# Writing the end of an output projection bank by bank, moving a table load, and adding squares before their row sums

## The chip, the cores and the metric

The kernel runs on 1 core of one Trainium2 chip. The metric is the device time of one execution in microseconds (us). A core has engines that run their own queues in order and wait for each other through semaphores: PE (matrix products, with PEld its weight loads), DVE (VectorE), ACT (ScalarE), POOL (GpSimd) and SP, which here only starts transfers.

## The reference, cut to what matters

Two model blocks follow each other over 256 tokens of width 1024. The first (attention, mLSTM, mixture of experts) is not touched by the change. The second has two layers; layer 0 is a gated linear attention ("gla"), layer 1 a state space layer ("s5"). Three places of it matter:

```
# layer 0: each of the 4 heads has 512 output columns; they are normed per token and head
o = gla_chunked(q, k, v, g)                       # (B, L, 4, 512)
o = o * rsqrt(mean(o * o, over 512) + EPS) * out_norm_w

# layer 1, after the state space scan (y is 256 x 2048)
y = gelu(y)
y = y * sigmoid(y @ w_glu + b_glu)                # w_glu 2048 x 2048
seq_out = y
...
y = concatenate([seq_out, xa]) * silu(z)          # 256 x 3072
x = x + y @ w_out                                 # w_out 3072 x 1024
return x * rsqrt(mean(x * x) + EPS) * final_norm_w
```

## The kernel before, in words

Everything is held transposed: features on the 128 partitions, the 256 tokens (T) along the free axis. A weight matrix comes in tiles of 1 MB (`load`, L262, issued by SP), and each half of a tile is split into a rounded part and a rest (`split`, L267 on ACT writes `whi`, L268 on DVE or POOL writes `wlo`); a product is then three passes through PE (`mm3`), left and right rounded part and both cross terms. Such products stand at L280, since `mm` records every one of them. The split halves rotate through four buffers (`ws`), the raw tiles through five. Sums pile up in PSUM, in eight banks that are handed out anew from stage to stage (`psum_banks`); the first product into a bank handed out anew waits until whoever read it last is done.

**The heads of layer 0** (L1518 to L1532). For each head `f` and each of its four blocks `e` of 128 columns, PE forms the block `po` in a bank (two products, `ps<-gatt,gv`), ACT squares it (`sq`, L1524) and DVE copies it out (L1525, into `gqk`, `gz` or `gG` by head). A product of the constant matrix `mean` with each square (`ps<-sq,c_ident`) adds the four up over the partitions in a bank `pm`. ACT takes the root (`gro`, L1528), DVE its reciprocal (L1529) and multiplies the four blocks by it (L1531). Behind the last head the banks are handed out anew and the projection `gx` starts (`ps<-hh,whi`).

**The output stage of layer 1** (from L1740). For each of eight groups PE applies the output table (`st<-Xs,tab`), DVE adds (L1747), ACT applies gelu (L1748), and the result goes out to DRAM and back in another order (`yd`, `yy`), is split again, and waits as an operand of `w_glu`. Between these PE already multiplies the tiles f = 16 to 23 of the output projection (`wout`, `acc<-gyh,whi` and the like: 24 products a tile, into four banks `acc`). Then for f = 0 to 15: 48 products of `w_glu` into a bank `ps`, ACT the sigmoid (L1781), DVE a product with the gate (L1782), the split into `gyh` and `gyl` (two buffers each), and one tile of the output projection, one f behind (`last`). Each tile goes through all four banks.

**The end.** When `acc` is complete, DVE adds each of the eight column blocks to the residual (L1792), ACT squares it (`yy`, L324), PE sums the squares (`st<-c_ident,yy`), POOL scales the block by the norm's weight (L1794); ACT takes the root (`rfc`, L333), DVE the reciprocal, PE spreads it over the partitions (`ps<-c_ident,rfc`), DVE multiplies (L1799) and four transfers take the result out.

`root_table` is a one-element root on ACT, whose only use is that ACT loads the table for roots at that place. A scheduler, not the order of the text alone, decides where each instruction stands in its engine's queue: what depends on nothing may stand far ahead. `tc.issue_after` holds the instructions in it behind a given one.

## Time and profile before

| what | value |
|---|---|
| time, median of 3 runs | 1500.61 us (1500.07 to 1500.84) |
| the profiled execution | 1499.36 us |
| its span, first to last instruction | 1497.3 us |
| PE busy | 1337.9 us (89%) |
| DVE busy | 761.6 us (51%) |
| ACT busy | 549.8 us (37%) |
| POOL busy | 323.3 us (22%) |
| mean granted clock of PE | 0.93 |

The span is read in stretches: the heads of layer 0 run from about 863 to 889 us, the output stage of layer 1 from about 1290 us, its loop over f from about 1345 us, and the end from about 1477 us. Busy shares over the whole span mix stages with different limits. Between the span and the time of the execution lie 2.1 us; the profiled execution lies 1.25 us below the median.

### The profile page before, as it was taken

The numbers are of one execution on the slowest core, as the hardware profiler recorded it, in microseconds if no ns is written. First come the engines' busy times: TensorE is split into PE (matmuls) and PEld (weight loads), VectorE is DVE, ScalarE is ACT, GpSimd is POOL, SyncE is SP. The second block draws the span as 40 slices with busy tenths as digits, with TensorE's granted clock in tenths as the row PEclk, the third lists the DMA queues.
The fourth block names the chain that finished last, engine by engine and source line by source line (L and its number), as shares of the span: only waits on it lengthen the run. The fifth ranks groups of instructions, "written<-read, shape, count | busy, mean of one in ns | idle before, by whom it ended". The sixth has DMA issues, their size and how long they took to land. (4 is left out here: it accounts for less than half of the span.)

```text
span 1497.3 us, 25797 instructions
## 1 busy us (share of the span) xinstructions
PE 1337.9 (89%) x10632; PEld 1065.1 (71%) x10632; DVE 761.6 (51%) x1498; ACT 549.8 (37%) x859; POOL 323.3 (22%) x450
## 2 busy tenths in 40 slices
PE   5999998987887888686679999999999999999997
PEld 2777796553454555341159989999888988999997
DVE  2766454812233321010047686588846899665553
ACT  3754553321211122110034435644522355444443
POOL 0031121412223231200008887111400000030001
PEclk8899999998988999896689999999999999999998
DMA  9776764999999999999994525889766534675540
GB/s 364 277 268 250 268 246 174 379 400 420 420 408 415 420 408 420 420 421 374 421 370 156 204 92 178 259 251 320 265 203 204 170 138 147 213 205 189 178 141 29
DMA packets 87626, 414.86 MB, mean 277 GB/s; under 512 B 26432, under 2 KB 28016, under 8 KB 43472
## 3 DMA queue, kind: packets, MB, share of 16 engines
q1 hardware_dynamic: 66768, 381.85, 66.9%
q0 software_dynamic: 8016, 22.13, 4.7%
q10 hardware_dynamic: 12720, 9.18, 1.9%
q8 instruction: 86, 1.41, 0.4%
q14 instruction: 36, 0.29, 0.1%
HBM read 392.90 MB, written 20.22 MB: 276 GB/s over the span
## 5 line engine op out<-in xcount | busy, mean ns | idle before, releaser
L267 ACT ACTIVATE whi<-w 128x1024 fp32r<-128x1024 f32 x252 | 263.7, 1056 | 329.8 <-PE ps L280 249.9
L268 DVE TENSOR_TENSOR wlo<-w,whi 128x1024 fp32r<-128x1024 f32 x222 | 273.4, 1240 | 145.2 <-ACT whi L267 144.6
L280 PE MATMUL ps<-hh,whi 128*128 128x256 f32 x928 | 272.8, 294 | 11.2 <-DVE zt L1614 5.0
L280 PE MATMUL ps<-hh,wlo 128*128 128x256 f32 x928 | 266.9, 288 | 2.0 <-DVE wlo L268 1.8
L280 PE MATMUL ps<-hl,whi 128*128 128x256 f32 x928 | 267.8, 289 | 0.9 <-DVE hl L1579 0.7
L280 PEld LDWEIGHTS ps<-hh,whi 128*128 128x128 f32 x928 | 179.0, 193 | 19.5 <-issue 9.1
L280 PEld LDWEIGHTS ps<-hh,wlo 128*128 128x128 f32 x928 | 178.8, 193 | 4.5 <-DVE wlo L268 2.6
L280 PEld LDWEIGHTS ps<-hl,whi 128*128 128x128 f32 x928 | 179.0, 193 | 2.0 <-DVE hl L1579 0.7
L280 PE MATMUL A<-w,xg 128*32 128x512 f32 x984 | 139.6, 667 | 33.8 <-DMA w<-in_w 32.9
L280 PE MATMUL acc<-gyl,whi 128*128 128x256 f32 x384 | 109.1, 284 | 0.6 <-DVE gyl L268 0.6
L280 PE MATMUL acc<-gyh,wlo 128*128 128x256 f32 x384 | 109.1, 284 | 0.0
L280 PE MATMUL acc<-gyh,whi 128*128 128x256 f32 x384 | 108.2, 282 | 0.0
L268 POOL TENSOR_TENSOR wlo<-w,whi 128x1024 fp32r<-128x1024 f32 x30 | 70.6, 2368 | 167.1 <-ACT whi L267 166.9
L934 DVE SCALAR_TENSOR_TENSOR xT<-m,mod,xT 128x256 f32<-128x256 f32 x64 | 27.8, 480 | 142.7 <-PE m L280 142.7
L280 PEld LDWEIGHTS A<-w,xg 128*32 128x32 f32 x984 | 23.8, 114 | 102.3 <-DMA w<-in_w 73.2
L280 PE MATMUL A<-w,gT 128*32 128x512 f32 x512 | 75.0, 687 | 24.1 <-DMA w<-in_w 16.5
L960 DVE TENSOR_TENSOR g<-g,A 128x512 f32<-128x512 f32 x8 | 5.5, 687 | 134.3 <-PE A L280 134.3
L280 PEld LDWEIGHTS acc<-gyl,whi 128*128 128x128 f32 x384 | 72.7, 189 | 1.5 <-DVE gyl L268 0.8
L280 PEld LDWEIGHTS acc<-gyh,whi 128*128 128x128 f32 x384 | 73.2, 191 | 0.2 <-issue 0.2
L280 PEld LDWEIGHTS acc<-gyh,wlo 128*128 128x128 f32 x384 | 72.9, 190 | 0.2 <-issue 0.2
L1759 POOL TENSOR_TENSOR zs<-zs,yy 128x256 f32<-128x256 f32 x16 | 14.7, 935 | 236.9 <-DMA yy<-yd 236.1
L280 PE MATMUL ps<-wlo,hh 128*128 128x256 f32 x192 | 56.1, 292 | 3.4 <-DVE wlo L268 3.4
(585 smaller groups left out, 2766.8 us busy)
## 6 DMA issues: line engine op xcount, KB each, us to landing
w<-in_w SPq DMA_DIRECT2D x187, 1024.0 KB, 11.5
w<-in_wada SPq DMA_DIRECT2D x24, 1024.0 KB, 7.3
w<-in_wo SPq DMA_DIRECT2D x24, 1024.0 KB, 5.3
w<-in_sglu SPq DMA_DIRECT2D x16, 1024.0 KB, 4.9
w<-in_gz SPq DMA_DIRECT2D x12, 1024.0 KB, 6.9
w<-in_sz SPq DMA_DIRECT2D x12, 1024.0 KB, 4.8
w<-in_win SPq DMA_DIRECT2D x10, 1024.0 KB, 7.1
w<-in_xk SPq DMA_DIRECT2D x8, 1024.0 KB, 9.7
```

Of the source, the lines that this page charges most:

```text
L267: self.nc.scalar.activation(hi, src, AF.Copy)
L268: (eng or self.nc.vector).tensor_sub(lo, src, hi.bitcast(F32))
L280: self.nc.tensor.matmul(ps, l, r, start=start, stop=stop, **kw)
L934: self.nc.vector.scalar_tensor_tensor(self.xT[:, f], pc[:, T * c:T * c + T], self.m(5)[:, f:f + 1], self.xT[:, f], op0=OP.mult, op1=OP.add)
L960: nc.vector.tensor_mul(g1, g1, p3)
L1759: nc.gpsimd.tensor_mul(zs[:, f], zs[:, f], u)
```

## The change

In the heads, the squares of one head are added up on DVE (three additions for four squares), and one product with `mean` per head takes the place of four. In the loop over f, the tiles f = 13, 14 and 15 of the output projection are held back until the last `w_glu` product and then written bank by bank, tile 15 one bank behind the others; their weights stay split (one half of them in the buffer `xa`), and `gyh` and `gyl` get a third buffer. `root_table` is held behind the last sigmoid.

```diff
--- before.py
+++ after.py
@@ -268,12 +268,15 @@
         (eng or self.nc.vector).tensor_sub(lo, src, hi.bitcast(F32))
         return hi, lo
 
-    def halves(self, src):
+    def halves(self, src, room=None):
 
         raw = self.load(src.rearrange("p a b c -> p (a b c)") if len(src.shape) == 4 else src.rearrange("p a b -> p (a b)"))
         for i in range(2):
-            hi = self.ws.tile([128, 1024], F32R, tag="whi", name="whi")
-            lo = self.ws.tile([128, 1024], F32R, tag="wlo", name="wlo")
+            if i and room is not None:
+                hi, lo = room[:, 0], room[:, 1]
+            else:
+                hi = self.ws.tile([128, 1024], F32R, tag="whi", name="whi")
+                lo = self.ws.tile([128, 1024], F32R, tag="wlo", name="wlo")
             yield self.split(raw[:, 1024 * i:1024 * i + 1024], hi, lo, self.nc.gpsimd if i < self.spread else None)
 
     def mm(self, ps, l, r, start, stop, **kw):
@@ -1383,6 +1386,12 @@
             cs = slice(128 * c, 128 * c + 128)
             self.mm3(o, [x[:, cs] for x in w], y, first and c % 2 == 0, last and c % 2 == 1, skip_group_check=True)
 
+    def wout_bank(self, acc, g, w, y, last):
+
+        for c in range(2):
+            cs = slice(256 * g + 128 * c, 256 * g + 128 * c + 128)
+            self.mm3(acc[g][:, T * c:T * c + T], [x[:, cs] for x in w], y, False, last and c == 1, skip_group_check=True)
+
     def gated(self, W, s, z):
 
         nc = self.nc
@@ -1520,10 +1529,14 @@
                     po = self.psum()[:, :T]
                     self.mm(po, v[:, 0, es], att[:, f, 0:256], True, False, skip_group_check=True)
                     self.mm(po[:, 128:], v[:, 1, es], att[:, f, 256:384], False, True, skip_group_check=True)
-                    sq = self.t(W, [128, T], "sq")
+                    sq = self.t(W, [128, T], "sq" if e else "gro")
                     nc.scalar.activation(sq, po, AF.Square)
                     nc.vector.tensor_copy(o[:, e], po)
-                    self.mm(pm, self.cp["mean"], sq, e == 0, e == 3)
+                    if e:
+                        nc.vector.tensor_add(sums, sums, sq)
+                    else:
+                        sums = sq
+                self.mm(pm, self.cp["mean"], sums, True, True)
                 ro = self.t(W, [128, T], "gro")
                 nc.scalar.activation(ro, pm, AF.Sqrt, bias=self.eps, scale=2.0)
                 nc.vector.reciprocal(ro, ro)
@@ -1761,13 +1774,18 @@
 
             def last(f, g, wo=[None]):
                 if f % 2 == 0:
-                    wo[0] = self.halves(io["wo1"][f // 2])
+                    wo[0] = self.halves(io["wo1"][f // 2], self.t(P, [128, 2, 1024], "xa", F32R) if f == 12 else None)
+                if f == 12:
+                    self.wout(acc, next(wo[0]), g, False, False)
+                    kept.append(next(wo[0]))
+                    return
                 self.wout(acc, next(wo[0]), g, f == 16, f == 15)
 
-            prev = None
+
+            prev, kept, lasty = None, [], []
             for f in (16, 17, 18, 19, 20, 21, 22, 23, 0, 1, 2, 3, 4, 5, 6, 7, 8, 9, 10, 11, 12, 13, 14, 15):
-                gh = self.t(W, [128, T], "gyh", F32R)
-                gl = self.t(W, [128, T], "gyl", F32R)
+                gh = self.t(W, [128, T], "gyh", F32R, bufs=3)
+                gl = self.t(W, [128, T], "gyl", F32R, bufs=3)
                 if f >= 16:
                     self.split(xa[:, f - 16], gh, gl)
                     last(f, (gh, gl))
@@ -1778,15 +1796,23 @@
                         self.mm3(ps, [x[:, 128 * k:128 * k + 128] for x in wg], [x[8 * (k % 2) + 4 * j + k // 2] for x in ys],
                                  j + k == 0, j + k == 8)
                 sg = self.t(W, [128, T], "sg")
-                nc.scalar.activation(sg, ps, AF.Sigmoid, bias=self.v("s5_b_glu_2", f))
+                gate = nc.scalar.activation(sg, ps, AF.Sigmoid, bias=self.v("s5_b_glu_2", f))
                 nc.vector.tensor_mul(sg, sg, zs[:, f])
                 self.split(sg, gh, gl)
                 if f == 15:
-                    self.root_table(W)
-                if prev:
+                    with tc.issue_after(gate.ins):
+                        self.root_table(W)
+                if prev and f < 14:
                     last(*prev)
+                if f >= 13:
+                    lasty.append((gh, gl))
                 prev = f, (gh, gl)
-            last(*prev)
+            kept += list(self.halves(io["wo1"][7]))
+            for g in range(5):
+                for i in range(3):
+                    b = g - (i == 2)
+                    if 0 <= b < 4:
+                        self.wout_bank(acc, b, kept[i], lasty[i], i == 2)
             ps = self.psum("st")[:, :2].rearrange("p (t n) -> p t n", t=2)
             for k in range(8):
                 nc.vector.tensor_add(x3[:, k], acc[k // 2][:, T * (k % 2):T * (k % 2) + T], x3[:, k])
```

On DVE, around the second head. `gqk0` and `gqk1` hold the blocks of heads one and two, `gz` those of head three; `ps_...` are banks, `gro` is a sum of squares or a root.

Before:

```order
L1529 RECIPROCAL gro_7430<-gro_7430 128x256
L1525 COPY gqk1_7398<-ps_7445 128x256
L1531 SCALAR_TENSOR_TENSOR gqk0_7397<-gqk0_7397,vec_74,gro_7430 128x256 x4
L1525 COPY gqk1_7398<-ps_7452 128x256
L1525 COPY gqk1_7398<-ps_7459 128x256
L1529 RECIPROCAL gro_7466<-gro_7466 128x256
```

After:

```order
L1542 RECIPROCAL gro_7430<-gro_7430 128x256
L1534 COPY gqk1_7398<-ps_7438 128x256
L1544 SCALAR_TENSOR_TENSOR gqk0_7397<-gqk0_7397,vec_74,gro_7430 128x256 x4
L1534 COPY gqk1_7398<-ps_7444 128x256
L1536 TENSOR_TENSOR gro_7441<-gro_7441,sq_7447 128x256
L1534 COPY gqk1_7398<-ps_7451 128x256
L1536 TENSOR_TENSOR gro_7441<-gro_7441,sq_7454 128x256
L1534 COPY gqk1_7398<-ps_7458 128x256
L1536 TENSOR_TENSOR gro_7441<-gro_7441,sq_7461 128x256
L1542 RECIPROCAL gro_7466<-gro_7466 128x256
```

Three additions have come in, the last of them directly ahead of the reciprocal of the same head. (Before, the head's first copy stands ahead of the first row shown.)

On PE, the last head and the first product of the projection behind it. In brackets stands whom the instruction waits for (DVE_49 is DVE, Activation_49 is ACT, PE_49 is PE itself).

Before:

```order
L280 MATMUL ps_7524<-gatt_6552,gv_6828 128x256 [waits DVE_49]
L280 MATMUL ps_7524<-gatt_6552,gv_6828 128x128
L280 MATMUL ps_7509<-sq_7520,c_ident_72 128x256 [waits Activation_49]
L280 MATMUL ps_7531<-gatt_6552,gv_6828 128x256
L280 MATMUL ps_7509<-sq_7527,c_ident_72 128x256 [waits Activation_49]
L280 MATMUL ps_7531<-gatt_6552,gv_6828 128x128
L280 MATMUL ps_7509<-sq_7534,c_ident_72 128x256 [waits Activation_49]
L280 MATMUL ps_7550<-hh_6437,whi_7553 128x256 [waits DVE_49,Activation_49]
```

After:

```order
L283 MATMUL ps_7473<-gro_7477,c_ident_72 128x256 [waits DVE_49,PE_49]
L283 MATMUL ps_7510<-gatt_6552,gv_6828 128x256 [waits PE_49]
L283 MATMUL ps_7510<-gatt_6552,gv_6828 128x128
L283 MATMUL ps_7516<-gatt_6552,gv_6828 128x256 [waits PE_49]
L283 MATMUL ps_7516<-gatt_6552,gv_6828 128x128
L283 MATMUL ps_7523<-gatt_6552,gv_6828 128x256 [waits Activation_49]
L283 MATMUL ps_7523<-gatt_6552,gv_6828 128x128
L283 MATMUL ps_7530<-gatt_6552,gv_6828 128x256 [waits PE_49]
L283 MATMUL ps_7530<-gatt_6552,gv_6828 128x128
L283 MATMUL ps_7509<-gro_7513,c_ident_72 128x256 [waits DVE_49,PE_49]
L283 MATMUL ps_7550<-hh_6437,whi_7553 128x256 [waits Activation_49]
```

The products with squares now come once a head, behind all its blocks and ahead of the next head's, and wait for DVE instead of ACT.

At the end, ACT from the last sigmoid on and PE's last rows. `rfc` is the root of the final norm, `st` the bank of its sums.

Before, ACT and then PE:

```order
L1781 ACTIVATE sg<-ps,vec 128x256
L267 ACTIVATE gyh<-sg 128x256
L324 ACTIVATE yy<-xT 128x256 x8
L333 ACT_TABLE_LOAD
L333 ACTIVATE rfc<-st,c_ident 128x2
L280 MATMUL acc<-gyh,wlo 128x256
L280 MATMUL st<-c_ident,yy 128x1 x16
L280 MATMUL ps<-c_ident,rfc 128x128 x2
```

After, ACT and then PE:

```order
L1799 ACTIVATE sg<-ps,vec 128x256
L342 ACT_TABLE_LOAD
L342 ACTIVATE root<-c_ident 128x1
L267 ACTIVATE gyh<-sg 128x256
L327 ACTIVATE yy<-xT 128x256 x8
L336 ACTIVATE rfc<-st,c_ident 128x2
L283 MATMUL acc<-gyh,wlo 128x256
L283 MATMUL st<-c_ident,yy 128x1 x16
L283 MATMUL ps<-c_ident,rfc 128x128 x2
```

The table load has moved from behind the squares to between the last sigmoid and the split that follows it (before, `root_table` had stood ahead of the first gelu); on PE the sums of squares stand behind all of `acc` as before.

## Rows read from the trace of the kernel before

**Rows 1.** The page's busy times over the whole span (engine, us busy, share, instructions).

```profile
PE 1337.9 (89%) x10632; PEld 1065.1 (71%) x10632; DVE 761.6 (51%) x1498; ACT 549.8 (37%) x859; POOL 323.3 (22%) x450
```

**Rows 2.** Busy time of each engine by stretch of the heads of layer 0: stretch, its length, busy us of PE, PEld, DVE, ACT and POOL with instructions, granted clock of PE (1.00 is 2.4 GHz, 0.50 is 1.2 GHz), share of DMA, GB/s.

```profile
878.00:884.00 6.00, 6.00 (x32) 4.97 (x31) 6.00 (x12) 2.71 (x7) 5.76 (x14) 1.00 0.07 25
884.00:890.00 6.00, 2.89 (x13) 2.25 (x12) 6.00 (x11) 0.86 (x2) 3.53 (x9) 0.85 0.22 87
```

**Rows 3.** DVE's instructions in order of time in the heads: start, us (of merged ones from the first's start to the last's end), line, operation, tile, count. An idle time would stand in brackets.

```profile
871.12 1.40 DVE L1525 COPY gqk<-ps 128x256 f32<-128x256 f32 x4
872.55 1.23 DVE L268 TENSOR_TENSOR wlo<-w,whi 128x1024 fp32r<-128x1024 f32 x1
873.69 0.42 DVE L1525 COPY gqk<-ps 128x256 f32<-128x256 f32 x1
...
885.99 1.69 DVE L1531 SCALAR_TENSOR_TENSOR gz<-gz,vec,gro 128x256 f32<-128x256 f32 x4
887.60 1.07 DVE L1525 COPY gG<-ps 128x256 f32<-128x256 f32 x3
888.60 1.74 DVE L1529 RECIPROCAL gro<-gro 128x256 f32<-128x256 f32 x1
```

**Rows 4.** PE's products in order of time, in the heads and at the start of the projection behind them (in brackets the idle time before a row and what ended it).

```profile
869.77 0.59 PE L280 MATMUL ps<-sq,c_ident 128*128 128x256 f32 x2
870.20 1.04 PE L280 MATMUL ps<-gatt,gv 128*128 128x128 f32 x6
...
885.55 0.70 PE L280 MATMUL ps<-sq,c_ident 128*128 128x256 f32 x2 [0.53 <-ACT sq L1524]
888.82 0.55 PE L280 MATMUL ps<-hh,whi 128*128 128x256 f32 x1 [2.58 <-DVE gG L1525]
...
890.03 0.41 PE L280 MATMUL ps<-hh,wlo 128*128 128x256 f32 x1
890.24 0.41 PE L280 MATMUL ps<-hh,whi 128*128 128x256 f32 x1
...
895.57 0.28 PE L280 MATMUL ps<-hh,whi 128*128 128x256 f32 x1
```

**Rows 5.** ACT's last square and last root of the heads, in order of time.

```profile
885.11 0.38 ACT L1524 ACTIVATE sq<-ps 128x256 f32<-128x256 f32 x1 [1.28 <-PE ps L280]
886.28 0.47 ACT L1528 ACTIVATE gro<-ps,c_ident 128x256 f32<-128x256 f32 x1 [0.79 <-PE ps L280]
```

**Rows 6.** Who waited for whom: all of PE's waits from 888 to 1084 us (us in total, times, longest), then the first row of the chain that ended last (start, us, what).

```profile
PE ps L280 <- DVE gG L1525: 2.6, 1, 2.6
PE ps L280 <- DVE hl L1579: 0.7, 1, 0.7
PE ps L280 <- ACT hh L1578: 0.2, 1, 0.2
...
1084.47 5.98 PE ps L280 x48
```

**Rows 7.** DVE's multiplications of the blocks by the reciprocal root (line, engine, operation, tile, count: min/median/max ns, first and last start), its products with two operands in SBUF in the next stage, and one row of POOL in order of time (in brackets the idle time before it).

```profile
L1531 DVE SCALAR_TENSOR_TENSOR gqk<-gqk,vec,gro x8: 541/646/678, 876.0 to 882.5; 128x256 f32<-128x256 f32 x8
L1531 DVE SCALAR_TENSOR_TENSOR gz<-gz,vec,gro x4: 472/472/501, 886.0 to 887.2; 128x256 f32<-128x256 f32 x4
L1390 DVE TENSOR_TENSOR gy<-gqk,zt x8: 417/422/620, 925.2 to 969.3; 128x256 f32<-128x256 f32 x8
888.20 0.40 POOL L1336 TENSOR_TENSOR s_t<-s_raw,a 128x128 f32<-128x128 f32 x1 [2.00 <-DMA tab<-s_t]
```

**Rows 8.** The start of the output stage of layer 1, in order of time: DVE's first addition, ACT's two table loads, PE's wait behind it.

```profile
1294.30 0.69 DVE L1747 TENSOR_TENSOR U<-st,U 128x512 f32<-128x512 f32 x1 [0.35 <-PE st L280]
1293.54 0.20 ACT L339 ACTIVATE root<-c_ident 128x1 f32<-128x1 f32 x1
1295.06 0.63 ACT L1748 ACTIVATE U<-U 128x512 f32<-128x512 f32 x1
1338.91 0.39 PE L280 MATMUL acc<-gyl,whi 128*128 128x256 f32 x1 [0.58 <-DVE gyl L268]
```

**Rows 9.** PE at the end, in order of time: the first product of the last two tiles, the sums of squares, the spreading of the root.

```profile
1477.12 0.28 PE L280 MATMUL acc<-gyh,whi 128*128 128x256 f32 x1
1477.24 0.28 PE L280 MATMUL acc<-gyl,whi 128*128 128x256 f32 x1
1482.88 4.43 PE L280 MATMUL st<-c_ident,yy 128*128 128x1 f32 x32
1487.87 1.22 PE L280 MATMUL ps<-c_ident,rfc 128*128 128x128 f32 x4 [0.55 <-DVE rfc L334]
```

**Rows 10.** ACT, DVE and POOL at the end, in order of time.

```profile
1477.38 0.48 ACT L1781 ACTIVATE sg<-ps,vec 128x256 f32<-128x256 f32 x1 [4.72 <-PE ps L280]
1478.42 0.42 ACT L267 ACTIVATE gyh<-sg 128x256 fp32r<-128x256 f32 x1 [0.56 <-DVE sg L1782]
1485.25 1.28 ACT L333 ACT_TABLE_LOAD   x1
1478.87 0.42 DVE L268 TENSOR_TENSOR gyl<-sg,gyh 128x256 fp32r<-128x256 f32 x1 [0.48 <-ACT gyh L267]
1489.20 2.48 DVE L1799 TENSOR_TENSOR xa<-xT,ps 128x512 f32<-128x512 f32 x4 [1.39 <-POOL xT L1794]
1481.96 7.25 POOL L1794 TENSOR_SCALAR xT<-xT,vec 128x256 f32<-128x256 f32 x8 [143.38 <-ACT yy L324]
```

## The prediction

> **What bounds the kernel now.** I read the busy shares of the whole span first: PE is busy for 89% of it and DVE for 51% [rows 1]. That says that PE bounds the kernel on average, and nothing about the three places that change, so I read each in its own stretch.
>
> In the heads of layer 0 the busy times by stretch show PE and DVE both full: 6.00 of 6.00 us each from 878 to 884 us [rows 2]. Both can't set the pace. A full PE is doubtful, since its rows overlap; DVE's are real: in order of time they stand without an idle bracket from 871.12 us until the last copy ends at 888.67 us [rows 3]. PE, in contrast, waits for a square (0.53 us) and then 2.58 us for DVE's last copy, and the projection behind the heads starts at 888.82 us [rows 4]. So DVE sets the pace, and the start of the projection is the end of DVE's list.
>
> What follows carries a delay on. From 888 to 1084 us PE waits only 0.9 us beside that first wait, and from 1084 us the chain that ended last runs on through PE and what feeds it [rows 6].
>
> At the end of the kernel PE goes without a gap from the output projection into the sums of squares, 4.43 us from 1482.88 us; then come the root and its spreading (1487.87 to 1489.09 us), and DVE's last products start at 1489.20 us [rows 9, 10].
>
> **The heads, additions.** Removed are 12 products with squares on PE, 0.43 us each by the start of the next row (869.77 to 870.20 us) [rows 4], 5.2 us in all. PE isn't the pace there, so this earns nothing. Added are 12 additions of 128x256 on DVE, which has no gap. The nearest rows of that form, with two operands in SBUF, take 0.42 us alone (0.62 at most) [rows 7]. Instructions in a row overlap a little: three copies of 0.42 us each take 1.07 us [rows 3], so an addition would cost 0.33 us at least: 4.0 us for 12. But POOL works on SBUF in this stretch, and the multiplications by the reciprocal root take 0.65 us beside it and 0.47 us when POOL stands still, as it does for 2.00 us before 888.20 us [rows 7]. POOL is busy most of the time [rows 2], so I add most of that 0.17 us, 0.12: 0.45 us, 5.4 us for 12. The upper bound is that each waits out one POOL instruction (0.40 us [rows 7]) on top of 0.35: 0.75 us, 9.0 us.
>
> The Trainium skill (SBUF — State Buffer, section Who interferes with whom) says that a VectorE instruction with two SBUF inputs contends with a GpSimd instruction that reads SBUF, and that the later one blocks fully. The trace agrees in sign (0.65 against 0.47 us); by the rule alone the 12 could come to the upper bound.
>
> **The heads, a new wait.** Before, DVE had other work between a head's last copy and its reciprocal, and four products were spread over the head. Now the reciprocal stands directly behind the third addition in DVE's queue, and the way is: addition, product with `mean` on PE, root on ACT, reciprocal. The same way is in the trace from the last square's end (885.49 us) to the root's end (886.75 us): 1.26 us with PE at 2.4 GHz [rows 5]. At 1.2 GHz the product's two passes take 0.43 us more, as the pitch of a product doubles (0.21 us at 890 us against 0.12 us) [rows 4, 9]. PE has about 3 us of work left in a head of more than 6 us, and in the trace the clock is at the lower level after 2.58 us without products, so I take the middle, 1.5 us. Queued behind the waiting reciprocal are the next head's copies. Head one: a weight split covers 1.14 us (872.55 to 873.69 us) [rows 3], which leaves 0.4. Heads two and three: 1.5 each. Head four: the projection's first product stands behind the last sum and waits for ACT's root, 1.5 us behind the last addition instead of 0.15 us behind the last copy, so 1.35. Sum 4.7 us; bounds 3.7 (2.4 GHz throughout) and 5.5 (1.2 GHz).
>
> The projection starts at 1.2 GHz before [rows 4]; it will again, so this is no term. Together the heads cost 10.1 us, between 7.7 and 14.5.
>
> **The output stage.** The early table load and root vanish ahead of the first gelu. That gelu starts at 1295.06 us, 0.07 us after DVE's addition ends, so it waited for DVE and the load was covered: nothing. The third `gyh` buffer lets splits run earlier; PE's one wait for such a split is 0.58 us [rows 8]. PE's queue also takes the groups in another order here, with their transfers. I take -0.5, between -1 and +1.
>
> **The end.** PE does the same 72 products in either order, and the sums of squares stand behind all of them as before. Their 4.43 us do not wait for the squares, so DVE's earlier additions and POOL's earlier scaling (POOL ends at 1489.21 us now [rows 10]) meet the same root: the spreading ends at 1489.09 us, and at most 0.1 us can be won. The load that moves was covered too: it ends at 1486.53 us, the sums at 1487.31 us [rows 9, 10]. In its new place it stands ahead of the last `gyh`. The last `w_glu` product now ends 2.88 us earlier; after it come sigmoid (ending 0.74 us behind), load 1.28, root 0.20 [rows 8, 10], `gyh` and `gyl` 0.45 each: 3.1 us. Four bank pieces of six products at 0.12 us cover 2.9, and `gyl` is wanted by the second product behind, at 3.0. A wait of some 0.2 us, between -0.1 and +0.5.
>
> **Sum.** 10.1 - 0.5 + 0.2 = +9.8 us. The profiled execution would go from 1499.36 to 1509.2 us; it lies 1.25 us below the median, so the median goes from 1500.61 to 1510.4 us.
>
> **The rivals.**
> Contention: each addition waits out a POOL instruction (9.0 us instead of 5.4), with the clock low in every wait: 14.5 - 0.5 + 0.2, 1514.8 us. For it speaks that POOL is busy 5.76 of 6 us [rows 2]; against it that the multiplications lose only 0.17 us.
> The other side: PE sets the pace of the heads, and DVE's rows only follow it. Then 12 products fewer take 5.2 us off, the later start of the projection gives 1.35 back: 1496.8 us. It decides if DVE's list per head with three additions still fits into what PE needs. For it speaks PE's 6.00 of 6.00 us; against it DVE's rows without a gap.
> Absorbed: something behind the heads, POOL's tables or a transfer, was late anyway and eats the delay: 1500 to 1503 us. Against it speaks that PE's waits up to 1084 us hold 0.9 us.
> The end pays: the row of DVE's last products names POOL as what it waited for [rows 10]. Were that the limit, POOL would end some 2.3 us earlier, with bank 0 complete 2.9 us earlier: 1508.1 us. Against it the spreading ends only 0.1 us before.
>
> **How the numbers follow.** Forecast 0.74, with 1506.5 to 1513.5 us as its own range; contention 0.11; the other side 0.06; absorbed 0.05; the end pays 0.04. A change of 0.2% (3 us) is about what a measurement of this kernel can tell from none. Faster 0.06, same 0.05, slower 0.89. The range 1505 to 1514.8 leaves out the other side, the absorbed case, half of contention and a little of the forecast's tails, some 0.18.
>
> **What would show it.** In the changed trace DVE's heads should hold 12 additions of 0.4 to 0.6 us and idle times of 1.2 to 1.8 us ahead of two reciprocals, named as waits for ACT; the projection should start near 899 us; PE's clock should be low in parts of the heads. The sums of squares at the end should again take 4.4 us or more, right behind `acc`. Wrong it would be if the reciprocals don't wait, if the additions disappear in gaps, or if the projection starts before 890 us.

## The result, and the profile after

The changed kernel takes 1509.66 us (median of 6 runs, 1509.2 to 1510.85); the kernel before, run beside it, 1500.72 us (6 runs). The ratio is 1.0062, with a 95% interval of 1.0042 to 1.0082: slower by 6.3 to 12.3 us. The profiled execution took 1509.2 us with a span of 1507.1 us. The forecast was 1510.4 us.

The page's busy times over the whole span, after (compare [rows 1]):

```profile
PE 1342.4 (89%) x10608; PEld 1067.4 (71%) x10608; DVE 764.5 (51%) x1510; ACT 548.8 (36%) x858; POOL 324.9 (22%) x450
```

PE has 24 instructions fewer (twelve products of two passes each) and DVE has 12 more. Nothing else in this row tells where 9 us went; the stretches do. DVE in order of time through the heads, after (compare [rows 3]; L1536 are the additions, L1542 the reciprocals, L1534 the copies):

```profile
868.73 0.74 DVE L1534 COPY gqk<-ps 128x256 f32<-128x256 f32 x2
869.48 0.42 DVE L1536 TENSOR_TENSOR gro<-gro,sq 128x256 f32<-128x256 f32 x1
...
870.16 0.65 DVE L1536 TENSOR_TENSOR gro<-gro,sq 128x256 f32<-128x256 f32 x1
...
873.35 1.75 DVE L1542 RECIPROCAL gro<-gro 128x256 f32<-128x256 f32 x1 [0.54 <-ACT gro L1541]
...
879.82 0.41 DVE L1536 TENSOR_TENSOR gro<-gro,sq 128x256 f32<-128x256 f32 x1
882.11 1.75 DVE L1542 RECIPROCAL gro<-gro 128x256 f32<-128x256 f32 x1 [1.88 <-ACT gro L1541]
...
887.30 0.41 DVE L1536 TENSOR_TENSOR gro<-gro,sq 128x256 f32<-128x256 f32 x1
889.08 1.75 DVE L1542 RECIPROCAL gro<-gro 128x256 f32<-128x256 f32 x1 [1.36 <-ACT gro L1541]
...
895.22 0.65 DVE L1536 TENSOR_TENSOR gro<-gro,sq 128x256 f32<-128x256 f32 x1
897.71 1.75 DVE L1542 RECIPROCAL gro<-gro 128x256 f32<-128x256 f32 x1 [1.84 <-ACT gro L1541]
```

Two things have come into a list that had no gap: additions of 0.41 to 0.70 us, and an idle bracket ahead of each of the four reciprocals, all four named as a wait for ACT's root. PE in the same stretch (compare [rows 4]):

```profile
871.62 1.19 PE L283 MATMUL ps<-gro,c_ident 128*128 128x256 f32 x2 [5.49 <-DVE gro L1536]
...
880.38 1.19 PE L283 MATMUL ps<-gro,c_ident 128*128 128x256 f32 x2 [3.54 <-DVE gro L1536]
...
887.86 0.67 PE L283 MATMUL ps<-gro,c_ident 128*128 128x256 f32 x2 [1.54 <-DVE gro L1536]
...
896.01 1.15 PE L283 MATMUL ps<-gro,c_ident 128*128 128x256 f32 x2 [4.86 <-DVE gro L1536]
897.73 0.58 PE L283 MATMUL ps<-hh,whi 128*128 128x256 f32 x1 [0.56 <-ACT gro L1541]
898.11 0.41 PE L283 MATMUL ps<-hl,whi 128*128 128x256 f32 x1
898.32 0.41 PE L283 MATMUL ps<-hh,wlo 128*128 128x256 f32 x1
...
903.67 0.28 PE L283 MATMUL ps<-hh,whi 128*128 128x256 f32 x1
```

The products with squares have become one row sum per head, which waits for DVE's last addition; 15.4 us of waiting in all. The row sum takes 0.67 us at the higher clock and 1.15 to 1.19 us at the lower. From DVE's first copy (868.73 us) to the projection's first product (897.73 us) are 29.0 us, against 17.7 us before (871.12 to 888.82 us [rows 3, 4]): +11.3 us. The projection again starts at the lower clock, with a pitch (start to start) of 0.21 us.

The same stretch by windows of 6 us (columns as in [rows 2]):

```profile
878.00:884.00 6.00, 3.62 (x11) 3.12 (x12) 4.12 (x8) 1.24 (x3) 5.45 (x12) 0.58 0.00 0
884.00:890.00 6.00, 4.46 (x21) 3.82 (x21) 4.64 (x12) 2.07 (x6) 3.26 (x8) 0.85 0.22 89
```

PE and DVE stood at 6.00 of 6.00 us each from 878 to 884 us [rows 2]; now neither does, and PE's granted clock is 0.58 where it was 1.00. Two engines that work less each and take longer together: they wait for each other in turn.

Behind the heads, all of PE's waits from 898 to 1094 us (compare [rows 6]; the second row is the projection's first wait, shown above, which the window cuts into):

```profile
PE ps L283 <- DVE hl L1592: 0.7, 1, 0.7
PE ps L283 <- ACT gro L1541: 0.6, 1, 0.6
```

There is no slack in which the delay could have been absorbed. The end of the kernel, DVE, then ACT, PE and POOL in order of time (compare [rows 9, 10]):

```profile
1489.49 0.76 DVE L1818 TENSOR_TENSOR xT<-acc,xT 128x256 f32<-128x256 f32 x2 [0.96 <-PE acc L283]
...
1493.81 1.48 DVE L1818 TENSOR_TENSOR xT<-acc,xT 128x256 f32<-128x256 f32 x4 [1.40 <-PE acc L283]
1500.79 2.48 DVE L1825 TENSOR_TENSOR xa<-xT,ps 128x512 f32<-128x512 f32 x4 [1.39 <-PE ps L283]
...
1485.78 0.48 ACT L1799 ACTIVATE sg<-ps,vec 128x256 f32<-128x256 f32 x1 [2.77 <-PE ps L283]
1486.27 1.28 ACT L342 ACT_TABLE_LOAD   x1
...
1494.33 4.58 PE L283 MATMUL st<-c_ident,yy 128*128 128x1 f32 x32
1499.46 1.23 PE L283 MATMUL ps<-c_ident,rfc 128*128 128x128 f32 x4 [0.55 <-DVE rfc L337]
...
1495.43 3.63 POOL L1820 TENSOR_SCALAR xT<-xT,vec 128x256 f32<-128x256 f32 x4 [0.92 <-ACT yy L327]
```

DVE's additions now start 4.8 us ahead of the sums of squares, and POOL is done 1.7 us ahead of DVE's last products instead of at the same moment. To DVE's last products this earned nothing: from the first sum they start 6.46 us later (1494.33 to 1500.79), against 6.32 us before (1482.88 to 1489.20 us [rows 9, 10]). To the execution it earned 1.6 us: from the first sum to the end of the span are 12.77 us, against 14.37 us before. What closes the span is a drain on POOL, an instruction of its queue that the busy times leave out. POOL's drains (duration min/median/max in ns, first and last start in us), before and then after:

```profile
L1836 POOLq DRAIN  x3: 40/113/11144, 1485.3 to 1497.0; - x3
L1862 POOLq DRAIN  x3: 40/113/9547, 1496.7 to 1506.8; - x3
```

The long one runs from 1485.3 to 1496.4 us before and from 1496.7 to 1506.3 us after. In both it ends 7.2 us behind POOL's last scaling (1489.21 us [rows 10] and 1499.06 us), and the span ends 0.84 us behind it. It is the same in all thirteen profiled executions: the span ends 8.05 to 8.09 us behind POOL's last scaling, and no other engine's closing drain ends later than POOL's. Where the output stage and the end are as before (seven kernels), DVE's last products start 5.0 to 6.3 us behind the first sum, and the span ends 14.35 to 14.40 us behind it all the same. So it is POOL's last scaling that the end waits for, and the change brought it forward. Why the drain takes that long is not shown.

### The profile page after: what moved, and what is told of

The parts are those of the page before. It is cut to its first block, busy times and chain, and to the rows that moved or that the text cites. A ratio compares the mean times of both kernels' runs of the same rounds, so it can differ in the third digit from the quotient of the medians.

```text
span 1507.1 us, 25754 instructions
## 1 busy us (share of the span) xinstructions
PE 1342.4 (89%) x10608; PEld 1067.4 (71%) x10608; DVE 764.5 (51%) x1510; ACT 548.8 (36%) x858; POOL 324.9 (22%) x450
## 5 line engine op out<-in xcount | busy, mean ns | idle before, releaser
L283 PEld LDWEIGHTS ps<-hh,whi 128*128 128x128 f32 x928 | 180.4, 194 | 17.5 <-issue 6.2
L283 PEld LDWEIGHTS A<-w,xg 128*32 128x32 f32 x984 | 23.8, 113 | 102.9 <-DMA w<-in_w 74.8
```

The costliest lines, as they stand in the source:

```text
L283: self.nc.tensor.matmul(ps, l, r, start=start, stop=stop, **kw)
```

## The experiments

Each run goes against the kernel before on the same chip. "Heads" is the time from DVE's first copy of a block (where ACT copies, from 0.14 us behind the start of the last copy into `gatt`, where DVE's first copy starts in the others) to the projection's first product, in the profiled execution. Single executions of one kernel differ by several us in stretches that no edit touches: DVE's first copy of the heads stands between 868.0 and 876.0 us over the profiled executions with copies on DVE. So a difference of stretches counts where its rows explain it, and the times are medians of 10 to 12 runs (6 of the changed kernel, one of e8).

What happens in the heads also shows in the clock at which the projection starts. In the kernel before, its products come at the lower clock first and at a pitch of 0.12 us from the 31st on, which is this one:

```profile
895.21 0.28 PE L280 MATMUL ps<-hh,whi 128*128 128x256 f32 x1
```

"31st" is therefore the time from the same first copy to the 31st product. From there to the 96th product all kernels take the same (7.7 us; e8 7.8). "Stretches" adds up what a kernel differs from the one before in the parts that its edit touches: up to the 31st product, and, where the later part of the change is in it, -1.9 us for output stage, loop over f and end (-2.3 us in e5 and e9; see the last sections). "Medians" is the difference of the two times.

| kernel | heads, us | 31st, us | stretches, us | medians, us | time, us | before beside it | ratio (95%) |
|---|---|---|---|---|---|---|---|
| before | 17.7 | 24.1 | | | | | 1 |
| after | 29.0 | 34.9 | +8.9 | +8.9 | 1509.66 | 1500.72 | 1.0062 (1.0042 to 1.0082) |
| e1 heads alone | 29.8 | 35.1 | +11.0 | +12.8 | 1513.24 | 1500.43 | 1.0082 (1.0057 to 1.0107) |
| e2 rest alone | 18.0 | 24.2 | -1.8 | -2.5 | 1497.91 | 1500.43 | 0.9980 (0.9958 to 1.0002) |
| e3 additions, unused | 24.5 | 30.9 | +6.8 | +6.5 | 1506.94 | 1500.43 | 1.0043 (1.0020 to 1.0066) |
| e4 one product a head | 17.5 | 23.8 | -0.3 | -0.1 | 1500.34 | 1500.43 | 0.9993 (0.9970 to 1.0016) |
| e5 rest, and additions at the end | 18.0 | 24.2 | -2.1 | -4.3 | 1497.00 | 1501.32 | 0.9977 (0.9955 to 0.9999) |
| e6 old banks for the projection | 13.7 | 18.1 | -6.0 | -6.3 | 1494.81 | 1501.15 | 0.9962 (0.9942 to 0.9983) |
| e8 additions from PSUM, unused | 23.9 | 28.8 | +4.7 | | 1503.48, one run | 1501.32 | |
| e9 e5, e6 and copies on ACT | 14.4 | 18.8 | -7.6 | -6.6 | 1494.74 | 1501.32 | 0.9966 (0.9945 to 0.9987) |
| e10 copies on ACT | 16.5 | 20.1 | -4.0 | -5.5 | 1495.86 | 1501.32 | 0.9971 (0.9951 to 0.9992) |
| e11 after, copies on ACT | 27.0 | 32.2 | +6.2 | +1.9 | 1503.09 | 1501.15 | 1.0006 (0.9983 to 1.0029) |
| e12 after, row sum later | 28.3 | 33.8 | +7.8 | +6.8 | 1507.90 | 1501.15 | 1.0048 (1.0026 to 1.0071) |

An interval of a ratio reaches some 3 to 4 us to either side. The stretches, read from one execution each, lie inside it for every kernel but e11.

### Which part carries it

The kernel before with the hunk of the heads alone, and with everything else alone:

```diff
 # e1: before, with
-                    self.mm(pm, self.cp["mean"], sq, e == 0, e == 3)
+                    if e:
+                        nc.vector.tensor_add(sums, sums, sq)
...
+                self.mm(pm, self.cp["mean"], sums, True, True)
```

```diff
 # e2: after, with
-                    if e:
-                        nc.vector.tensor_add(sums, sums, sq)
...
+                    self.mm(pm, self.cp["mean"], sq, e == 0, e == 3)
```

> The kernel before with the heads' edit alone (three additions and one product per head). My theory, that the heads carry the whole loss: slower by 9 to 11 us, about 1510 to 1511 us, with idle times of 1.3 to 1.9 us ahead of the reciprocals of heads two and three. Rival, that the loss comes from the later stages (tiles held back, load moved) or is spread: slower by less than 6 us.

> The changed kernel with the heads as before (tiles bank by bank, the load behind the last sigmoid, three buffers). My theory: -0.3 us, the same within 0.1%, the first of DVE's last products some 6.3 us behind the start of the sums of squares as before. Rival, that the end pays because DVE and POOL start earlier: faster by 2.3 us.

The heads alone give the whole slowdown (1.0082; up to the 31st product +11.0 us, as much as the +10.8 us of the whole change; I had expected 9 to 11 us), the rest alone at most a little gain (0.9980, its interval just reaching 1). In e2's trace the heads take 18.0 us. From its first sum of the end to the last products are 5.99 us, against 6.32 us before, as I had expected; but from that sum to the end of the span are 12.77 us, 1.6 us less than before. With 0.5 us of the output stage and 0.2 us lost in between, the rest gains 1.9 us. So the time came nearer to the rival (2.3 us faster) than to my 0.3 us. The interval alone would not decide it; the rows of POOL do.

### The additions without the wait

Twelve additions whose result nothing reads; the four products with squares per head stay:

```diff
 # e3: before, with
+                    if e == 1:
+                        sums = self.t(W, [128, T], "gro")
+                    if e:
+                        nc.vector.tensor_add(sums, sq, sq)
```

```diff
 # e8: the same, with one operand in PSUM
+                        nc.vector.tensor_add(sums, po, sq)
```

> The kernel before with twelve additions of the same form beside the copies, whose result nobody reads; the four products per head stay. It prices the additions without the new wait. My theory: slower by 5 to 6 us (twelve at some 0.47 us each), no idle time ahead of the reciprocals. Rival, that the additions fit into gaps and the wait is everything: no change. Rival, contention: slower by 9 us.

> The kernel before with twelve additions in the heads whose result nothing reads, as in the run with unused additions, but one of the two operands is in PSUM (the block itself) and not in SBUF. Theory (the additions with both operands in SBUF take 0.6 to 0.7 us where GpSimd works at the same time, 0.41 us where it is still, since both use SBUF): with one operand in PSUM each takes about 0.4 us also beside GpSimd, and the heads (from the first block's copy to the projection's start, 17.7 us before, 24.5 us with the unused SBUF additions) take 17.7 + 12 x 0.41 = 22.6 us. Rival (the additions are slow where GpSimd works, whatever they read): the heads take about 24.5 us again. Rival (a fixed 0.35 us pitch as with the copies): 21.9 us.

The additions of e3, of e8 and of the changed kernel (duration min/median/max in ns, first and last start in us):

```profile
L1529 DVE TENSOR_TENSOR gro<-sq x12: 407/617/702, 869.5 to 892.4; 128x256 f32<-128x256 f32 x12
```

```profile
L1529 DVE TENSOR_TENSOR gro<-ps,sq x12: 406/410/425, 870.2 to 892.5; 128x256 f32<-128x256 f32 x12
```

```profile
L1536 DVE TENSOR_TENSOR gro<-gro,sq x12: 408/420/702, 869.5 to 895.2; 128x256 f32<-128x256 f32 x12
```

e3 adds 6.8 us to the heads without the row sum's wait (0.23 us of idle time ahead of the last reciprocal is all there is): additions alone make the kernel slower, on an engine that has no gap. I had expected 5 to 6 us. What the change has above that, 29.0 less 24.5, is 4.5 us. e3's additions take 6.0 us by the starts of the rows behind them, those of the change 5.5 us, so some 5 us are left for the new wait, which the rows of the changed kernel put at 5.5 us.

e8 tells what slows an addition down. With both operands in SBUF the median is 617 ns and eight of twelve take over 600; with one in PSUM none takes over 425 ns, though POOL works through the same stretch in both. Three of e3's four additions of 0.41 us start from 884.21 to 885.55 us, where POOL is idle until 885.20 us; beside the third an instruction of POOL takes 0.66 us for a usual 0.40. So contention is real, either engine can be the one delayed, and the delay is a part of an instruction of POOL (0.2 to 0.3 us of 0.40), not a whole one each time. The time of e8's heads missed, though: 23.9 us, not 22.6. Its additions cost 4.1 us, but three waits of 0.36 to 0.47 us came with them, perhaps because an addition that reads the block in its bank holds that bank longer; no run shows that. Some 0.8 us stays without an account.

### What sets the pace of the heads

One product with `mean` per head, of the last block's square alone: the squares of three blocks of four are left out of the norm.

```diff
 # e4: before, with
-                    self.mm(pm, self.cp["mean"], sq, e == 0, e == 3)
+                self.mm(pm, self.cp["mean"], sq, True, True)
```

> The kernel before with one product per head and no additions (left out: the squares of three of the four blocks in each head's norm). It takes 5.2 us off PE and adds nothing to DVE. My theory, that DVE sets the pace of the heads: the same within 1 us, the projection starting some 17.7 us behind DVE's first copy as before. Rival, that PE sets the pace: faster by 4 to 5 us.

PE in e4 in order of time, the start of the projection:

```profile
888.28 0.55 PE L280 MATMUL ps<-hh,whi 128*128 128x256 f32 x1 [6.29 <-DVE gG L1525]
```

The twelve products less give nothing: the heads take 17.5 us, the time is that of before (0.9993), and PE's wait for DVE's last copy is 6.29 us instead of 2.58 us [rows 4]. DVE's list, not PE's products, was the path, which the row of busy shares could not tell [rows 2].

Two edits then shorten what DVE's list holds up:

```diff
 # e6: before, with
-            self.psum_banks(acc=4, ps=2, at=2)
             xa = self.t(P, [128, 8, T], "hf")
             for b in range(4):
+                if b == 2:
+                    self.psum_banks(acc=4, ps=2, at=2)
                 ps = self.dense_t(io["gx"][b], h)
```

```diff
 # e10: before, with
-                    nc.vector.tensor_copy(o[:, e], po)
+                    nc.scalar.activation(o[:, e], po, AF.Copy)
```

> The kernel before, with one line moved: the projection behind the heads uses the heads' PSUM banks for its first two blocks, so that its first product no longer waits for VectorE's last copy of the last head. Theory (that wait, 2.58 us in the kernel before, is a stop of TensorE on the path, and the low clock that the trace shows behind it is its consequence): the projection starts at about 15.1 to 15.5 us behind the first copy in place of 17.7, its first products come at 0.12 us each and not at 0.21, and the time falls by 2.2 to 5 us, to 1495.5 to 1498.3. Rival (the projection's results wait for the heads' blocks on VectorE anyway): the start is earlier but the time within 1.5 us of before.

> The kernel before with the sixteen copies of the heads' blocks on ScalarE in place of VectorE. Theory (VectorE's instructions, end to end, set the pace of the heads): sixteen copies by 0.35 us leave VectorE, 5.6 us; ScalarE takes them in its gaps until its own sum (16 squares by 0.38, 16 copies by about 0.38, four roots by 0.47 and a table of 1.28, about 15.3 us) is nearly the length of the heads. The heads fall from 17.7 to 13 to 15 us, the time to about 1496.5 to 1498.5 (ratio 0.9975 to 0.9985). Rival (ScalarE becomes the bound, or the chain of square, row sum, root, reciprocal does): the heads stay at 16.5 to 18 us and the time within 1.5 us of before. Rival (the squares and copies in one queue keep TensorE's banks longer): heads over 18 us, time above before.

PE in e6 at the same place, and its window from 884 to 890 us:

```profile
887.60 0.38 PE L280 MATMUL ps<-gatt,gv 128*128 128x128 f32 x2
887.74 0.37 PE L280 MATMUL ps<-hh,whi 128*128 128x256 f32 x1
887.94 0.28 PE L280 MATMUL ps<-hl,whi 128*128 128x256 f32 x1
888.06 0.28 PE L280 MATMUL ps<-hh,wlo 128*128 128x256 f32 x1
```

```profile
884.00:890.00 6.00, 5.94 (x35) 4.99 (x33) 6.00 (x13) 2.36 (x6) 4.12 (x9) 1.00 0.23 90
```

The projection's first products follow the last block's product without a bracket, at a pitch of 0.12 us from the second on, and the granted clock of that window is 1.00, against 0.85 before [rows 2]. The heads fall by 4.0 us, more than the expected 2.2 to 2.6, since the projection starts even ahead of the last two squares' products. The time falls by 6.3 us (its interval reaches from 2.6 to 8.7 us). The clock carries the difference: PE does not stop ahead of the projection, its products come at the higher level, and at the 31st (892.14 us in e6) the gain is 6.0 us. From there on it stays at 6.0 us, so the rival by which the projection's results wait for DVE anyway falls.

e10 fell short in the heads: 16.5 us, not 13 to 15, the edge of the rival by which ACT or the chain becomes the bound. Its time fell by 5.5 us, and here too the clock is part of it: PE waits only 0.56 us ahead of the projection (2.58 us before), the products come at 0.12 us, and by the 31st the gain is 4.0 us. DVE's reciprocals now wait for ACT's root:

```profile
871.80 1.75 DVE L1529 RECIPROCAL gro<-gro 128x256 f32<-128x256 f32 x1 [1.56 <-ACT gro L1528]
...
885.35 1.75 DVE L1529 RECIPROCAL gro<-gro 128x256 f32<-128x256 f32 x1 [1.01 <-ACT gro L1528]
```

With 5.6 us less on DVE (sixteen copies by 0.35 us) its list has gaps, and the chain of square, row sum and root is what is late next.

### Where the same additions pay

The squares of parts 0 to 5 of the final norm are added on DVE, which has time there, and PE sums three squares instead of eight:

```diff
 # e5: e2, with
-                self.square_sums(W, k, x3[:, k], self.cp["mean"][:, 0:1], ps, tag="yy", bufs=4)
+                if k == 0:
+                    tot = q
+                elif k < 6:
+                    nc.vector.tensor_add(tot, tot, q)
```

> The kernel before with the output stage and the end of the change, its heads as before, and at the very end the squares of parts 0 to 5 summed on VectorE (five additions of 128x256) ahead of TensorE, which then sums three squares in place of eight. Theory (in the heads the addition costs because VectorE is full there and TensorE is not; at the end VectorE is idle and TensorE's sums of squares take 4.4 to 4.6 us in 32 half-speed products): TensorE's group of 32 falls to 12, 4.5 us to about 1.7 us, the five additions at 0.4 us hide between ScalarE's squares, and from TensorE's first sum of the end to the last scaling it is about 2.3 us shorter than in the kernel before (6.3 us there). In all 1500.4 - 0.5 - 2.3 + 0 = about 1497.6. Rival (an addition costs wherever it stands, since the sums then wait for the additions): that stretch stays at 6 us or more, and the time within 1 us of 1500.

PE at the end of e5:

```profile
1482.74 0.28 PE L283 MATMUL acc<-gyh,wlo 128*128 128x256 f32 x1
1484.63 0.58 PE L283 MATMUL st<-c_ident,sg 128*128 128x1 f32 x4 [1.61 <-DVE sg L1820]
1485.07 1.09 PE L283 MATMUL st<-c_ident,yy 128*128 128x1 f32 x8
1486.71 1.22 PE L283 MATMUL ps<-c_ident,rfc 128*128 128x128 f32 x4 [0.55 <-DVE rfc L337]
```

PE's 4.1 to 4.6 us of sums became 0.58 and 1.09 us, as expected, but PE now waits 1.61 us for the last addition. From the end of `acc` (1482.86 us by pitch) to DVE's last products (1488.04 us) are 5.2 us, against e2's 5.99: 0.8 us gained, not 2.3. The saving is real and two thirds of it went into the same kind of wait that the heads got: bank, residual, square, addition, sum, one behind the other. Of the 0.8 us the execution keeps 0.4 (12.41 us from the end of `acc` to the end of the span, against 12.77 us in e2), since POOL's last scaling closes it, and that came forward by as much only; two of POOL's scalings take 1.15 us beside the new additions in place of 0.92 us. The times of e5 and e2 (0.9977 and 0.9980) can't tell such a difference.

### The wait itself

The changed kernel with its copies on ACT, and with the row sum and what follows it issued behind the second block of the next head:

```diff
 # e11: after, with
-                    nc.vector.tensor_copy(o[:, e], po)
+                    nc.scalar.activation(o[:, e], po, AF.Copy)
```

```diff
 # e12: after, with row sum, root, reciprocal and scaling in scale()
+                    if e == 1 and late:
+                        scale(*late)
+                late = o, sums
+            scale(*late)
```

> The changed kernel with the sixteen copies of the heads' blocks on ScalarE in place of VectorE. Theory (of the 11.3 us that the heads grew about 6 are additions on a full VectorE and about 5 the wait for row sum, root and reciprocal): with 5.6 us off VectorE the additions find room in part, but the wait of each head stays since its chain is the same, so the heads fall by 3 to 5.6 us, from 29.0 to 23.5 to 26 us, still 6 or more above the 16.5 us of the kernel before with the same copies on ScalarE; time 1504 to 1507. Rival (the additions alone cost, through VectorE's length): heads 18 to 20 us and the time at that of the kernel before. Rival (the chain alone sets the pace now): heads 28 to 29 us, time as after.

> The changed kernel with the row sum, root, reciprocal and scaling of a head issued behind the first two blocks of the next head, so that TensorE, ScalarE and VectorE have those blocks to work on while the chain runs; every addition and operation of the change is still done. Theory (the wait ahead of the reciprocals, 0.54, 1.88, 1.36 and 1.86 us, is the chain's length, with nothing queued ahead of it): the first three waits go, the last one stays, and the heads fall from 29.0 to 25 to 25.7 us, about the 24.5 us of the run with unused additions plus the last wait; time about 1505.5 to 1506.5. Rival (the growth is all in the additions and in TensorE's low clock): heads 28 to 29.5 us. Rival (the wait moves to ScalarE's squares, whose buffers the scaling now holds): heads 26 to 28 us.

DVE in e11 and then in e12:

```profile
883.54 1.75 DVE L1542 RECIPROCAL gro<-gro 128x256 f32<-128x256 f32 x1 [1.88 <-ACT gro L1541]
886.07 0.43 DVE L1536 TENSOR_TENSOR gro<-gro,sq 128x256 f32<-128x256 f32 x1 [0.78 <-ACT sq L1533]
```

```profile
875.77 2.15 DVE L1531 SCALAR_TENSOR_TENSOR gqk<-gqk,vec,sq 128x256 f32<-128x256 f32 x4
877.84 0.62 DVE L1545 TENSOR_TENSOR gro<-gro,sq 128x256 f32<-128x256 f32 x1
...
879.05 0.49 DVE L1545 TENSOR_TENSOR gro<-gro,sq 128x256 f32<-128x256 f32 x1
...
879.80 0.70 DVE L1545 TENSOR_TENSOR gro<-gro,sq 128x256 f32<-128x256 f32 x1
881.29 1.75 DVE L1529 RECIPROCAL sq<-sq 128x256 f32<-128x256 f32 x1 [0.79 <-ACT sq L1528]
```

In e11, with 5.6 us off DVE, the heads fall by only 2.0 us: DVE's idle times ahead of reciprocals and additions add up to 8.0 us, against 5.6 us after. So once the additions are in, the chain sets the pace and a lighter DVE list mostly turns into waiting; the heads came out between what I expected (23.5 to 26 us) and the rival (28 to 29 us). The time fell by more than the heads explain (1503.1 us against 1509.7 us; 2.8 us by the 31st product). Of its profiled execution another 4.6 us lie in the layer behind the 31st product, where no instruction differs; the granted clock does (1.00 from 1050 to 1100 us, against 0.90 in the changed kernel's execution). But that layer moves by as much between executions of other kernels too, and medians should even it out, so why e11's time is this low, and what moves that clock, is left open.

e12 missed: 28.3 us, not 25 to 25.7. By the number alone the rival that knows only additions and a low clock (28 to 29.5 us) would have it, but the waits have not gone. The waits ahead of the reciprocals are still 0.88, 0.79, 1.23 and 1.94 us, 4.8 us in all. The first now holds the root's table load (1.28 us), which has come to stand behind the row sum. For the others the rows show why. A head's third and fourth addition stand in DVE's queue behind the scaling of the head before it (877.84 us, right behind 875.77 + 2.15), so the last addition ends at 879.54 us, and between it and the reciprocal stands about 1 us of work for a chain of 1.75 us (879.54 to 881.29 us). ACT's squares too wait for the scaling, whose buffers they now share (1.76 us and 3.38 us for `gqk` and `gz`), as the last rival said. Two blocks are too little cover here. A kernel with deeper cover was not run, so that the wait can be hidden whole is not shown.

### All that helped, together

> A kernel from what the runs showed: heads of the kernel before (no additions), their copies on ScalarE, the projection behind the heads using the banks of the heads for its first two blocks so that it does not wait for the last copy, the output stage and end of the change, and the end's squares of parts 0 to 5 summed on VectorE. Theory (each part earns where the engine it relieves is the one that is full): heads 17.7 to about 12 to 14 us (3.7 to 5.7 less), output stage 0.5 less, end 2.3 less, in all 1500.4 - 6.5 to 8.5 = about 1492 to 1494 (ratio 0.9945 to 0.9957). Rival (TensorE's clock takes it back: a projection that starts earlier runs longer at 1.2 GHz): heads shorter but the projection behind them longer by as much, time 1497 to 1498.

e9 is e5 with the edits of e6 and e10. Its time is 1494.74 us (0.9966), short of the 1492 to 1494 us that I expected and the same as that of e6 alone (1494.81 us, 0.9962). The heads take 14.4 us against 13.7 us in e6, and at the 31st product e9 has gained 5.3 us, e6 6.0 us: once the projection need not wait for the last copy, a lighter DVE gave nothing more. PE stood at 6.00 and 5.95 of 6.00 us from 876 to 888 us, so it may set the pace there; that is argued, not shown. The 2.3 us of the later stages are in e9's trace, but the intervals of the two times are too wide to find them. The intervals of e5, e6, e9 and e10 all lie below 1; e6 gets there with one moved line.

## Why the prediction was right

**What bounds the heads.** It said that DVE's list without gaps sets the pace and PE's full share is misleading. e4 and e6 show it from both sides: 12 products off PE move nothing, and a projection that needn't wait for the list's last copy starts 4.0 us sooner.

**Additions, 5.4 us.** The twelve additions take 5.5 us by the starts of the rows behind them (1.24, 1.59, 1.08 and 1.55 us for the heads). The forecast was 0.45 us each, between 0.33 and 0.75 us; the rows run from 0.41 to 0.70 us. The surcharge for POOL, taken from the multiplications' 0.65 against 0.47 us [rows 7], had the right size on average. It is not a constant: an addition takes 0.41 us or 0.6 to 0.7 us. In the changed kernel each of the five slow ones starts 0.03 to 0.04 us behind the start of an instruction of POOL; others that run beside POOL stay at 0.41 us.

By the rule of the Trainium skill (SBUF — State Buffer, Who interferes with whom) the port pair that the two engines share is an exclusive lock, and the order of issue decides who blocks. The case agrees that the two interfere, that one operand in PSUM avoids it (410 ns in e8) and that either engine can be the later one (0.66 for 0.40 us on POOL). What an addition lost was less than what was left of the other's instruction: the one at 870.16 us lost 0.24 us to an instruction of POOL that started at 870.13 us and took 0.40 us. My upper bound, a whole POOL instruction for every addition, went beyond it.

**The new wait, 4.7 us.** It measured 5.5 us: 0.54, 1.88 and 1.36 us, and 1.71 us for the last (1.86 us from the last addition's end, 895.87 us, to 897.73 us, in place of the 0.15 us before). That is the upper bound of the range given for it; of the terms of the heads it is the one that was mis-sized. I took the middle between the two clock levels, and the lower held in three heads of four. I had read too little from the list of what is queued behind: on PE, the next head's products stand behind the row sum, so PE waits 3.5 to 5.5 us ahead of three of the four row sums, and these three ran at the lower level (1.15 to 1.19 us); behind a wait of 1.54 us the row sum took 0.67 us. The chain was also longer than forecast at either level: 1.37 us at the higher (third head) for 1.26, and 1.88 us at the lower (second head) for 1.69.

**The heads, +10.1 us.** +11.3 us: 5.5 and 5.5, and 0.3 us elsewhere, such as a weight split of 1.42 us for 1.23. By the 31st product it is +10.8 us, since the lower clock ends five products sooner than before; the prediction had this as no term.

**The output stage, -0.5 us.** PE's first `st<-Xs,tab` to its first product of `w_glu`: 1302.23 to 1355.92 us after, 53.69 us, against 54.16 us before (1290.48 to 1344.64 us), and PE's wait of 0.58 us for `gyl` [rows 8] is gone from the waits of that stretch. Both the size and the third buffer as its cause are borne out: the wait stands in the traces of all seven kernels with two buffers (0.2 to 2.5 us) and in none of the six with three. No run did the buffer alone.

**The end, +0.2 us: here the prediction was wrong.** Up to the first sum of squares it held. From that first product to the sum are 138.41 us (1355.92 to 1494.33 us) against 138.24 us (1344.64 to 1482.88 us): +0.17 us, and the same two numbers stand in all six and all seven kernels. The predicted wait for `gyl` behind the moved load shows as one pitch of 0.19 instead of 0.12 us. Behind that sum it said that POOL's earlier scaling meets the same root and that at most 0.1 us can be won. That holds for DVE's last products. But the span does not wait for them; it waits for POOL, whose last scaling came 1.6 us nearer to the first sum. So the term was -1.4 us.

**The rivals.** "Contention" as a whole waited-out instruction falls (e3, e8). "The other side" falls (e4). "Absorbed" falls: behind the projection's start PE waits 0.7 us up to 1094 us. "The end pays" does not fall. It asked whether POOL is the limit of DVE's last products; POOL is the limit of what comes behind them, and its earlier end paid 1.6 us where the rival had 2.3.

The sum, +9.8 us, met a difference of spans of +9.8 us (1497.3 to 1507.1 us). That is luck, as the stretches show:

| stretch | forecast, us | after less before, us |
|---|---|---|
| ahead of the heads | 0 | -2.4 |
| first copy to the projection's 31st product | +10.1 | +10.8 |
| from there to the output stage | 0 | +3.3 |
| output stage | -0.5 | -0.5 |
| loop over f, to the first sum of squares | +0.2 | +0.2 |
| from that sum to the end of the span | 0 | -1.6 |

The first and third rows hold nothing that the change touches; from the 31st product to the output stage the thirteen executions take from 393.8 to 400.5 us. The other four come to +8.9 us, which is also the difference of the medians. The forecast was 0.9 us above that, with the heads too small by 0.7 us and the end too large by 1.6 us.

## What to carry to other kernels

Where two engines both read as full, find the one whose rows stand in order without an idle bracket and whose end releases the next stage; here, work taken from the other earned nothing, and work put on it cost its full length. Adding operands ahead of a reduction trades products spread over a stage for one product behind all of them, whose wait every in-order queue then carries: look at what stands behind it. When a stage's last copy releases a bank for the next stage, let the next stage start in banks that are free already; here that gave as much as taking 5.6 us off the list (1494.8 and 1495.9 us). And at the end of a kernel, look for the engine whose end the execution closes behind: the instruction that finishes the result need not be it.

## What the runs showed of the hardware

A VectorE addition of 128x256 with both operands in SBUF takes 0.41 us alone and up to 0.61 to 0.70 us beside GpSimd's 128x128 instructions (e3, the changed kernel), with one operand in PSUM 0.41 to 0.43 us throughout (e8); GpSimd's own instruction can be the one delayed (0.66 for 0.40 us).

GpSimd's closing drain ended 7.21 us behind its last scaling in all thirteen executions, and later than the closing drain of any other engine.

The granted clock of PE in a stretch that no edit touches differs between executions. From 1050 to 1100 us, first in the changed kernel's execution and then in e1's:

```profile
1050.00:1100.00 50.00, 46.74 (x351) 46.13 (x350) 37.11 (x55) 23.97 (x38) 19.62 (x32) 0.90 0.77 265
```

```profile
1050.00:1100.00 50.00, 46.58 (x388) 45.98 (x387) 44.02 (x67) 27.33 (x43) 18.26 (x32) 1.00 0.85 287
```

With PE equally busy (46.7 and 46.6 us) the clock is 0.90 and 1.00, and the latter does more instructions (388 against 351) in the same time. Between the heads and the output stage the executions differ by nearly 7 us (393.8 to 400.5 us from the 31st product on), so differences of a few us need medians, or stretches that hold no such part.
